# A planned one-core matmul with tanh-gelu: next groups' needs first, another inner split in raw group two, P7 for P3 in group four

## The chip, the cores and the metric

The kernel runs on one core of one Trainium2 chip. The metric is device microseconds of one execution. Matrix products run on TensorE (PE, with PEld for its weight loads), element-wise work on VectorE (DVE) and ScalarE (ACT), and DMAs are issued by two queues: GpSimd's (POOL) for loads and SyncE's (SP) for stores. Operands lie in SBUF (the names `bR`, `aT`, `aD`, `stage`, `y`), products accumulate in eight PSUM banks (`acc`), and `k_unit`, `k_piece` and `park` are scratch in DRAM.

## The reference

```python
a, b: float32 [4096, 4096]
x = np.matmul(a, b)
out = 0.5 * x * (1 + np.tanh(np.sqrt(2 / np.pi) * (x + 0.044715 * x**3)))   # float32 [4096, 4096]
```

## The kernel before

**Tiling.** A and B are halved in both directions (quadrants 11, 12, 21, 22). The output is made in 16 groups: one of four row blocks of 512 rows (`mb`) with one of four column blocks of 512 columns (`nb`), in each of the four output quadrants. A group is a 2 x 2 block product with inner length 2048, done with seven products in place of eight (Winograd's form of Strassen's scheme). `P1` to `P7` are these products, all in fp16 with float32 sums: P1 and P2 make C11, P6 is added to P1, P7 and P5 complete C22, P4 completes C21, P3 completes C12. A plain product is four quarters of 16 matmuls of 128x512. A product can be cut: the same scheme is applied once more inside it, in seven parts of 256 columns and four stages (`split`, `stage`, `part_pe`, lines 973 to 1093). That takes fewer matmul cycles, and more sums on DVE and copies on ACT.

**Stages.** Group 0 is written out by hand. Groups 1 to 5 (`raw_group`, line 1424) read B from the input; `RAW_CUT` (line 97) says which products of each are cut: P3 in 1, 2 and 4, P7 in 5. Group 3 also turns to the next row block: it loads A's next rows in eight pieces, transposes them on DVE and squares each row on ACT with an accumulator (`turn_quad`, line 1249, the squares at line 1272) for a check of the inputs' sizes. Groups 6 to 15 run in pairs (`late_pair`) with all products cut. The squares of B's quadrants for the same check (`square`, line 1303: ACT at 1316, DVE at 1321) are made where `SQUARES` (lines 2002 and 2003) has the group and quadrant.

**Banks and buffers in a raw group.** X is the first four PSUM banks, Y the last four. After P6 each bank of X is copied to SBUF (`u2`, by `copy_out`, line 1230), and then P7 is accumulated on it. With P7 plain, `u3` copies it again, adds Y and sends C22 out. With P7 cut, P4 goes to Y alone and alternates with P7's stages, and `p7_out` (line 1571) reads each X bank twice: with `u` for C21 and with `v` into a new small buffer for C22. Gelu runs on ACT (`out_of`, line 1214), the store on SP (`store_out`, line 1219), and the buffer returns to the list. `new_small` takes the buffer that has been in the list longest; ten of them rotate in the raw groups. If both P7 and P3 are cut, `raw_group` returns P3 (`third`), and the next group alternates its four stages with the four quarters of its P1.

**Order.** Nothing is issued directly. `Plan.add` records each operation with its engine, a duration out of a table, what it reads and writes, and a due time: the planned PE time plus `slack`, moved ahead of those that depend on it (`Plan.keys`). `front` is the number of the first matmul group (one `add` on PE) that needs the operation's result. `Plan.schedule` (line 236) then walks through time. PE's order is fixed; every other engine takes, of the operations that are ready, the one with the least

```python
(not x.size and x.front > n_pe + FRONT, x.key, x.n)
```

where `n_pe` is the number of PE groups started and `size` is set for DMAs alone. Before it takes an operation, it looks for one that becomes ready while that one would run and that is due sooner (`near`). `emit` then issues all in the planned order, so each engine's queue is fixed when the program is built.

Of the kernel before, what the change touches and what calls it, by code (L numbers as in the profile page):

```python
# [93 lines left out]

N_RAW = 6
RAW_MAKES = {}
RAW_CUT = {1: "P3", 2: "P3", 4: "P3", 5: "P7"}
GROUPS = {
    6: modes_of(m="P1 P2 P3 P4 P5 P6 P7"),
    7: modes_of(m="P1 P2 P3 P4 P5 P6 P7"),  # L100
# [10 lines left out]
FROM_INPUT = ((0, "P2"), (1, "P1"), (1, "P2"), (1, "P3"), (2, "P3"), (3, "P3"))  # L111
OWN = True
TEMPS = ()
SLACK = 60.0
TURN_PLAN = (("11", "11", "P1", None), ("21", "12", "S4", None), ("12", "S1", "P5", None), ("22", "S2", "next", "P1"))
BEHIND = 4
FRONT = 0
CASTS = {4: ((1, 'P3'), (2, 'P3')), (8, 'P5'): ((0, 'P2'),)}
CAST_SLACK = 60.0
TURN_PLAN = (("11", "11", "P1", None), ("21", "12", "S4", None), ("12", "S1", "P5", None), ("22", "S2", "next", "P1"))  # L120
BEHIND = 4
FRONT = 0
CAST_BACK = 17
SLACK2 = 18.0
TURN_SLACK = 18.0
FILL_SLACK = 60.0
TURN_PLAN = (("11", "11", "P1", None), ("21", "12", "S4", None), ("12", "S1", "P5", None), ("22", "S2", "next", "P1"))
BEHIND = 4
FRONT = 0
CASTS = {4: ((1, 'P3'), (2, 'P3')), (8, 'P5'): ((0, 'P2'),)}  # L130
CAST_SLACK = 60.0
TURN_PLAN = (("11", "11", "P1", None), ("21", "12", "S4", None), ("12", "S1", "P5", None), ("22", "S2", "next", "P1"))
BEHIND = 4
FRONT = 0
CAST_BACK = 17
SLACK2 = 18.0
PARK = (6, 8, 10, 12, 14)
TURNS = {6: 2, 10: 3}
ORDER = "10 11 70 71 20 21 60 61 50 51 30 31 40 41"
# [17 lines left out]
class Plan:  # L157

    def __init__(self):
        self.ops, self.state, self.now = [], {}, BUSY["PE"]  # L160

    def add(self, eng, dur, fn, r=(), w=(), size=0, batch=None, after=(), slack=18.0, weight=1.0, every=None):
        o = Op()
# [72 lines left out]
    def schedule(self):  # L236
# [23 lines left out]
        while n_done < len(self.ops):  # L260
            best, at = None, 1e30
            if n_pe < len(pe) and not pe[n_pe].left:
                at = max(free["PE"], pe[n_pe].ready)
                best = "PE"
            for e in engines:
                if ready[e] and out.get(e, 0) < LANES:
                    t = max(free[e], min(o.ready for o in ready[e]))
                    if t < at:
                        best, at = e, t
            ended = self.next_move(at)  # L270
            if ended is not None:
                o, q = ended
                out[q] -= 1
                if o is not None:
                    o.end = self.moved + 0.4
                    finish(o)
                if out[q] == LANES - 1:
                    free[q] = max(free[q], self.moved + 0.4)
                continue
            assert best is not None  # L280
            if best == "PE":
                o = pe[n_pe]
                n_pe += 1
# [67 lines left out]
def half_path(  # L351
# [15 lines left out]
    W = 2 * NC  # L367
# [653 lines left out]
    def stage(z, k):  # L1021
# [38 lines left out]
        elif k == 3:  # L1060
            part_pe(z, "6")
            if z.last and not z.base:
                x6 = z.sum.pop("6")
                z.sum["3"] = inner_sum(-1, x12, as_inner(x6), x6)
            j2 = new_small()
            for r in range(2):
                copy_part(j(j2, r), of("21", r))
            part_pe(z, "7")
            for r in range(2):
                add_part(of("12", r), of("12", r), j(j2, r))  # L1070
            free_small.append(j2)
            for r in range(2):
                add_part(of("22", r), of("21", r), j(z.j5, r))
            free_small.append(z.j5)
# [142 lines left out]
    def store_out(gi, i, ih, jh, f):  # L1217
        r0, c0 = place(gi, i, ih, jh)
        dma("SP", out[r0 : r0 + P, c0 : c0 + NC], sm(f), [("f", f)], [], "out")
        free_small.append(f)  # L1220

    def out_from(gi, i, ih, jh, s):
        f = new_small()
# [25 lines left out]
    def turn_quad(mb, quad, slot, pairs, own=False, after=()):  # L1249
# [3 lines left out]
        for h in range(2):  # L1253
# [21 lines left out]
                    [] if own else toks, [("rows", ih), *(toks if own else [("f", f)])], batch=("w", mb, quad, h),  # L1275
                    slack=SLACK)
            if not own:
                free_small.append(f)
# [145 lines left out]
    def raw_group(gi, keep_units, makes, fetch=(), next_nb=None, turn=None, pending=None):  # L1424
# [164 lines left out]
        if "P7" in cut:  # L1589
# [41 lines left out]
    def more_smalls():  # L1631
        for x in EXTRA:
            free_cells.remove(x)
            for h in range(2):
                f = len(small)
                small.append(cell(x)[:, h * W : (h + 1) * W].bitcast(F32))
                free_small.append(f)
# [43 lines left out]
    def late_pair(ga, turn):  # L1681
# [64 lines left out]
        def split_pair(name, done):  # L1746
# [46 lines left out]

            def join(hw, f):
                into_bank(f, *of(hw[:2], int(hw[2])))
                free_small.append(f)

            def ended(hw, r):
                done(*of(hw, r))
# [129 lines left out]
        def p4_done(w, i):  # L1929
# [15 lines left out]
            for h in range(2):  # L1945
# [9 lines left out]
            free_small.append(f)  # L1955

        def park():
            for w, i in BANKS:
                f = u[w, i]
                dma("SP", parked[w][i][:, :], sm(f), [("f", f)], [("park", w, i)], "out")  # L1960
                free_small.append(f)

        def unpark():
            for w, i in BANKS:
# [9 lines left out]
        if last:  # L1974
            final_answer()
        both("P2", is_cut("P2"), p2_done)
        both("P6", is_cut("P6"), p6_done)
        if last:
            final_read()
# [14 lines left out]
        new_a("P4")  # L1994
        if turn:
            new_a("next")
            at.update(new, S1=at["S3"], S2=at["22"])
# [115 lines left out]
```

## Time and profile before

| | us |
|---|---|
| median of 3 runs | 1457.21 |
| lowest, highest | 1456.33, 1457.86 |
| profiled execution, its own time | 1458.38 |
| its span, first to last instruction | 1456.8 |

The mean granted clock of the profiled execution is 0.998. In the page, a group row gives the line, the engine, the operation, out<-in by the program's names, the count, then busy us and mean ns of one, then the engine's idle time before it and what ended most of it. Lines are those of helpers where a helper records the operation: all DMAs of the plan are at L822, all sums at L916, plain matmuls at L596, those of cut products in raw groups at L1001 and in pairs at L1780. The "chain" is the work that ended last, followed back in time. By that chain the group 1 starts at some 123 us, group 2 at 215, group 3 at 310, group 4 at 412, group 5 at 507, and the pairs at 604.

### The profile page before, as it was taken

To read this page: it belongs to the slowest core of one execution; us is meant where nothing else is said; L and a number is where in the kernel's file an instruction comes from. 1 tells how busy PE (TensorE), PEld (TensorE's weight loads), DVE (VectorE), ACT (ScalarE), POOL (GpSimd) and SP (SyncE) were. 2 spreads that over 40 slices of the span, in tenths; PEclk is the share of its full clock that TensorE was granted. 3 is DMA by queue.
4 is the path that set the end of the run, shared out by engine and by line. 5 is a ranking of instruction groups with operands and counts; after the bars stand their busy time and mean duration, and the time that the engine had idled before them with its cause. 6 is when DMAs were issued, how large, how long until landed. Compare 5 with 4: busy or idle time off the path is not lost.

```text
span 1456.8 us, 19885 instructions
## 1 busy us (share of the span) xinstructions
PE 1442.1 (99%) x6878; PEld 673.2 (46%) x6878; DVE 1192.0 (82%) x1280; ACT 698.3 (48%) x1460; POOL 488.3 (34%) x892
## 2 busy tenths in 40 slices
PE   8999999999899999999999999999999999999998
PEld 3444454454344545544444444444444444444443
DVE  2499987948477779889998989888999899887887
ACT  5546764553983543462554513435473623343133
POOL 7775351343334522341413343213232212221220
PEclk9999999999999999999999999999999999999999
DMA  9999999999999998998989899969998866875763
GB/s 170 196 196 240 311 270 267 236 292 253 208 222 268 231 312 231 256 281 286 287 320 307 264 295 326 288 227 310 257 347 270 275 257 218 319 265 199 272 251 125
DMA packets 205244, 378.91 MB, mean 260 GB/s; under 512 B 21073, under 2 KB 115793, under 8 KB 205137
## 3 DMA queue, kind: packets, MB, share of 16 engines
q0 software_dynamic: 146816, 245.42, 69.5%
q1 hardware_dynamic: 58320, 132.15, 24.2%
q8 instruction: 56, 0.92, 0.2%
q14 instruction: 52, 0.42, 0.1%
HBM read 333.45 MB, written 138.42 MB: 324 GB/s over the span
## 4 chain that ended last, share of the span: by engine, by line
PE 92%; DMA 3%; POOL 2%; ACT 1%; issue 1%; DVE 0%; DVEq 0%; ACTq 0%; POOLq 0%
PE acc L1780 58%; PE acc L596 31%; PE acc L1001 3%; DMA stage<-in_a_dram 2%; DMA bR<-in_b_dram 1%; POOL bR L498 1%; POOL stage L498 1%; ACT y L1272 1%; POOL aD L498 0%; PE acc L631 0%; DMA bR<-k_unit 0%; ACT y L1230 0%; DMA aD<-in_a_dram 0%; DVE bR L916 0%; DVE y L610 0%
## 5 line engine op out<-in xcount | busy, mean ns | idle before, releaser
L1780 PE MATMUL acc<-bR 128*128 128x512 f16 x1536 | 339.4, 379 | 1.4 <-DVE bR L916 1.4
L916 DVE TENSOR_TENSOR bR<-bR 128x2048 f16<-128x2048 f16 (+1 forms) x155 | 258.1, 1681 | 48.4 <-PE acc L1780 16.1
L822 POOL DMA_DIRECT2D bR<-k_unit x234 | 127.2, 545 | 468.6 <-PE acc L1780 358.4
L1780 PEld LDWEIGHTS <-bR 128*128 128x128 f16 x1776 | 173.7, 98 | 211.2 <-issue 1.7
L596 PE MATMUL acc<-bR,aT 128*128 128x512 f16 x1152 | 254.3, 381 | 2.5 <-ACT y L1230 2.5
L1780 PE MATMUL acc<-bR,aT 128*128 128x512 f16 x1008 | 223.6, 379 | 0.0
L822 POOL DMA_DIRECT2D bR<-in_b_dram x256 | 138.3, 546 | 214.8 <-DVE stage L916 74.9
L1780 PEld LDWEIGHTS <-aT 128*128 128x128 f16 x1344 | 131.5, 98 | 158.6
L596 PE MATMUL acc<-bR,aD 128*128 128x512 f16 x896 | 195.0, 379 | 1.9 <-ACT y L1230 1.9
L1792 ACT COPY acc<-acc 128x512 f32<-128x512 f32 x140 | 79.8, 570 | 241.8 <-PE acc L1780 221.2
L1236 DVE TENSOR_TENSOR y<-acc,y 128x512 f32<-128x512 f32 x239 | 158.5, 684 | 41.0 <-PE acc L1780 17.1
L596 PEld LDWEIGHTS <-aT 128*128 128x128 f16 x1216 | 119.3, 98 | 144.4 <-issue 5.3
L596 PEld LDWEIGHTS <-aD 128*128 128x128 f16 x992 | 96.9, 98 | 119.8 <-issue 2.9
L1316 ACT ACTIVATE y<-bR 128x1024 bf16<-128x1024 f16 x128 | 128.0, 1048 | 43.3 <-DVE y L1321 32.6
L1780 PE MATMUL acc<-bR,aD 128*128 128x512 f16 x624 | 138.4, 379 | 0.0
L1214 ACT ACTIVATE y<-y 128x512 f32<-128x512 f32 x156 | 95.5, 628 | 73.1 <-DVE y L1236 72.6
L1780 PEld LDWEIGHTS <-aD 128*128 128x128 f16 x784 | 76.7, 98 | 92.5
L1321 DVE TENSOR_TENSOR y<-y 128x1024 bf16<-128x1024 bf16 x120 | 81.6, 686 | 36.8 <-ACT y L1316 33.8
L1789 ACT COPY y<-acc 128x512 f32<-128x512 f32 x99 | 57.9, 585 | 93.9 <-PE acc L1780 84.7
L471 DVE STREAM_TRANSPOSE aT<-stage 128x1024 uint32<-128x1024 uint32 (+1 forms) x41 | 52.0, 1301 | 47.2 <-DMA stage<-in_a_dram 43.2
L1780 PE MATMUL acc<-stage,aT 128*128 128x512 f16 x336 | 75.6, 379 | 0.0
L1241 DVE TENSOR_TENSOR acc<-acc,y 128x512 f32<-128x512 f32 x100 | 68.7, 692 | 6.4 <-ACT y L1789 5.8
(120 smaller groups left out, 1579.1 us busy)
## 6 DMA issues: line engine op xcount, KB each, us to landing
bR<-k_unit POOLq DMA_DIRECT2D x234, 512.0 KB, 7.5
out_dram<-y SPq DMA_DIRECT2D x204, 256.0 KB, 7.3
bR<-in_b_dram POOLq DMA_DIRECT2D x352, 128.0 KB, 7.0
k_unit<-bR SPq DMA_DIRECT2D x76, 512.0 KB, 7.0
stage<-in_a_dram POOLq DMA_DIRECT2D x96, 256.0 KB, 8.8
stage<-k_unit POOLq DMA_DIRECT2D x46, 512.0 KB, 8.1
k_unit<-stage SPq DMA_DIRECT2D x28, 512.0 KB, 5.5
out_dram<-bR SPq DMA_DIRECT2D x46, 256.0 KB, 7.6
```

The lines of the kernel that those rows point to most:

```text
L471: nc.vector.transpose(dst[:, :, x, :], src)
L596: nc.tensor.matmul(acc, sa[:, j // 2, i * P : (i + 1) * P, j % 2], sb[:, j, :], start=start and j == 0, stop=stop and j == 3, skip_group_c ...
L822: return plan.add(queue, COST[queue], lambda: eng.dma_start(out=dst, in_=src), r=r, w=w, size=MOVE[what] * SPREAD, weight=weight, **kw)
L916: nc.vector.tensor_tensor(out=dst, in0=xa, in1=ya, op=ALU.add if op > 0 else ALU.subtract)
L1214: act("gelu", lambda: nc.scalar.activation(t, t, ACT.Gelu_apprx_tanh), [("f", f)], [("f", f)])
L1236: dve("add", lambda: nc.vector.tensor_tensor(out=sm(g), in0=bank(s, i), in1=sm(f), op=ALU.add), [("f", f)], [("f", g), ("p", s, i)])
L1241: dve("add", lambda: nc.vector.tensor_tensor(out=bank(s, i), in0=bank(s, i), in1=sm(f), op=ALU.add), [("f", f)], [("p", s, i)])
L1316: act("square", lambda t=t, src=src: nc.scalar.activation(t, src, ACT.Square), [c(cx)], [("f", f)], slack=60.0)
L1321: dve("add16", lambda t=t, u=u: nc.vector.tensor_tensor(out=u, in0=u, in1=t, op=ALU.add), [("f", f)], [("f", e)], slack=60.0)
L1780: nc.tensor.matmul(bank(w, i), sa[:, jx // 2, r * P : (r + 1) * P, jx % 2], bv[:, jx, :], start=p in "17" and jx == 0, stop=jx == NJ - 1, ...
L1789: act("copy", lambda: nc.scalar.copy(out=sm(f), in_=bank(w, i)), [("p", w, i)], [("f", f)])
L1792: act("copy", lambda: nc.scalar.copy(out=bank(*dst), in_=bank(*x)), [("p", *x)], [("p", *dst)])
```

## The change

Which products are cut: group 2 cuts P7 and P3, group 4 cuts P7 and no more P3. Since both are cut in group 2, its P3 runs within group 3. The order: `FRONT` is 2, so operations that one of the next three matmul groups needs go ahead of others; `near` also takes an operation that the next group needs (`NEAR = 0`) while the chosen one isn't needed by then; slacks and the place of the cast loads (`CAST_BACK`) have other values. The squares of B's quadrant 21 move from group 4 to group 3. `new_small` can lend halves of operand cells when the list is empty; `LEND` is empty, and `drop_small` stands in place of the plain return to the list. Constants that stood several times stand once.

```diff
-RAW_CUT = {1: "P3", 2: "P3", 4: "P3", 5: "P7"}
+RAW_CUT = {1: "P3", 2: "P7 P3", 4: "P7", 5: "P7"}
...
-SLACK = 60.0
+SLACK = 90.0
...
-FRONT = 0
+FRONT = 2
+LEND = ()
+SQUARES_3 = ("12", "21")
+NEAR = 0
...
-CAST_BACK = 17
-SLACK2 = 18.0
-TURN_SLACK = 18.0
+CAST_BACK = 9
+SLACK2 = 20.0
+TURN_SLACK = 12.0
...
     def halves(self, toks):
+        toks = [self.alias.get(t[:2], t) for t in toks]
...
-                o = min((x for x in ready[best] if x.ready <= at),
-                        key=lambda x: (not x.size and x.front > n_pe + FRONT, x.key, x.n))
+                def rank(x):
+                    return not x.size and x.front > n_pe + FRONT, x.key, x.n
+
+                o = min((x for x in ready[best] if x.ready <= at), key=rank)
                 if not o.size:
-                    near = [x for x in ready[best] if at < x.ready < at + o.dur and x.key < min(o.key, at + o.dur)]
+                    near = [
+                        x for x in ready[best] if at < x.ready < at + o.dur
+                        and (x.key < min(o.key, at + o.dur) or x.front <= n_pe + NEAR < o.front)
+                    ]
                     if near:
-                        o = min(near, key=lambda x: (x.key, x.n))
+                        o = min(near, key=rank)
                         at = max(at, o.ready)
...
-    def new_small():
+    lent = {}
+
+    def new_small(lend=False):
+        own = [f for f in free_small if f in lent]
+        if lend and own:
+            free_small.remove(own[0])
+            return own[0]
+        if not free_small or lend and len(free_cells) > 1:
+            x = new_cell()
...
         return free_small.pop(0)
+
+    def drop_small(f):
+        if f in lent and lent[f][1] in free_small:
+            free_small.remove(lent[f][1])
+            free_cells.append(lent[f][0])
+        elif f in lent:
+            free_small.append(f)
+        else:
+            free_small.insert(len([x for x in free_small if x not in lent]), f)
...
-            f = new_small()
+            f = new_small(i in LEND)
             add_bank(v[i], X, i, f)
             out_of(gi, i, 1, 1, f)
...
-            run(fourth, stages_of(split(X, s3, here(s12), True), p7_out))
+            if "P4" in cut:
+                run(fourth)
+                run(stages_of(split(X, s3, here(s12), True), p7_out))
+            else:
+                run(fourth, stages_of(split(X, s3, here(s12), True), p7_out))
...
             if "P3" in cut:
                 for i in range(RT):
                     add_bank(u[i], Y, i)
+                if turn:
+                    free_cells.extend(SB)
                 run(p4(X, False, p4_out), third())
+                if turn:
+                    for x in SB:
+                        free_cells.remove(x)
+                p4_ends()
                 load_next("12", "21")
...
-    SQUARES |= {(3, "12")} | {(4, q) for q in ("11", "21", "22", "end")}
+    SQUARES |= {(3, q) for q in SQUARES_3} | {(4, q) for q in ("11", "21", "22", "end") if q not in SQUARES_3}
```

More of the change, by code (lines that the diff above doesn't have):

```diff
@@ L113 @@
 TEMPS = ()
-SLACK = 60.0
+SLACK = 90.0
 TURN_PLAN = (("11", "11", "P1", None), ("21", "12", "S4", None), ("12", "S1", "P5", None), ("22", "S2", "next", "P1"))
 BEHIND = 4
-FRONT = 0
+FRONT = 2
+LEND = ()
+SQUARES_3 = ("12", "21")
+NEAR = 0
 CASTS = {4: ((1, 'P3'), (2, 'P3')), (8, 'P5'): ((0, 'P2'),)}
 CAST_SLACK = 60.0
-TURN_PLAN = (("11", "11", "P1", None), ("21", "12", "S4", None), ("12", "S1", "P5", None), ("22", "S2", "next", "P1"))
-BEHIND = 4
-FRONT = 0
-CAST_BACK = 17
-SLACK2 = 18.0
-TURN_SLACK = 18.0
-FILL_SLACK = 60.0
[L127 to L136, printed above, removed]
+CAST_BACK = 9
+SLACK2 = 20.0
+TURN_SLACK = 12.0
+FILL_SLACK = 60.0
 PARK = (6, 8, 10, 12, 14)
@@ L159, in __init__ @@
     def __init__(self):
-        self.ops, self.state, self.now = [], {}, BUSY["PE"]
+        self.ops, self.state, self.now, self.alias = [], {}, BUSY["PE"], {}
     def add(self, eng, dur, fn, r=(), w=(), size=0, batch=None, after=(), slack=18.0, weight=1.0, every=None):
@@ L845, in new_chunk @@
         return x
-    def new_small():
-        return free_small.pop(0)
+    lent = {}
[6 more added lines that the diff above has]
+            x = new_cell()
+            for h in range(2):
+                f = len(small)
+                small.append(cell(x)[:, h * W : (h + 1) * W].bitcast(F32))
+                plan.alias["f", f] = ("c", x, h)
+                free_small.append(f)
+            lent[f], lent[f - 1] = (x, f - 1), (x, f)
+            if lend:
+                return free_small.pop()
+        return free_small.pop(0)
+    def drop_small(f):
[3 more added lines that the diff above has]
+        elif f in lent:
+            free_small.append(f)
+        else:
+            free_small.insert(len([x for x in free_small if x not in lent]), f)
     def sm(f):
@@ L1070, in stage @@
                 add_part(of("12", r), of("12", r), j(j2, r))
-            free_small.append(j2)
+            drop_small(j2)
             for r in range(2):
                 add_part(of("22", r), of("21", r), j(z.j5, r))
-            free_small.append(z.j5)
+            drop_small(z.j5)
             z.prepare(3)
@@ L1219, in store_out @@
         dma("SP", out[r0 : r0 + P, c0 : c0 + NC], sm(f), [("f", f)], [], "out")
-        free_small.append(f)
+        drop_small(f)
     def out_from(gi, i, ih, jh, s):
@@ L1277, in turn_quad @@
             if not own:
-                free_small.append(f)
+                drop_small(f)
         if (mb, ih) in seen_rows:
@@ L1636, in more_smalls @@
                 small.append(cell(x)[:, h * W : (h + 1) * W].bitcast(F32))
-                free_small.append(f)
+                drop_small(f)
                 for r in range(2):
@@ L1795, in join @@
                 into_bank(f, *of(hw[:2], int(hw[2])))
-                free_small.append(f)
+                drop_small(f)
             def ended(hw, r):
@@ L1954, in p4_done @@
                 dma("SP", out[r0 : r0 + P, c0 + h * HC : c0 + (h + 1) * HC], t, [("f", f, h)], [], "out_half")
-            free_small.append(f)
+            drop_small(f)
         def park():
@@ L1960, in park @@
                 dma("SP", parked[w][i][:, :], sm(f), [("f", f)], [("park", w, i)], "out")
-                free_small.append(f)
+                drop_small(f)
         def unpark():
@@ L1976, in late_pair @@
         both("P2", is_cut("P2"), p2_done)
+        new_a("P2")
         both("P6", is_cut("P6"), p6_done)
@@ L1996, in late_pair @@
             new_a("next")
+            assert len(new) == 4
             at.update(new, S1=at["S3"], S2=at["22"])
```

## The prediction

> **What bounds the kernel now.** I read the profile page first, then the waits of PE, then the chain of waits, then busy time by stretches.
>
> ```profile
> span 1456.8 us, 19885 instructions
> PE 1442.1 (99%) x6878; PEld 673.2 (46%) x6878; DVE 1192.0 (82%) x1280; ACT 698.3 (48%) x1460; POOL 488.3 (34%) x892
> PE 92%; DMA 3%; POOL 2%; ACT 1%; issue 1%; DVE 0%; DVEq 0%; ACTq 0%; POOLq 0%
> ```
>
> PE is the bound: busy 99% of the span and 92% of the chain. So the time can fall in two ways only: fewer PE cycles, or fewer PE stops. The stops are few, and the waits of PE name all of them (engine, line, releaser, us in total, times, longest):
>
> ```profile
> PE acc L596 <- ACT y L1230: 4.4, 2, 2.5
> PE acc L631 <- DMA bR<-in_b_dram: 2.2, 2, 1.3
> PE acc L605 <- DVE table L777: 1.5, 1, 1.5
> PE acc L1780 <- DVE bR L916: 1.4, 1, 1.4
> ```
>
> The second and third rows lie in the hand-written first group, which is not edited. The first is the one that the change aims at. The chain shows what happens there: ACT's copies of a finished PSUM bank (L1230) stand behind row squares (L1272, a square and an accumulator read to each).
>
> ```profile
> 366.59 0.73 ACT y L1272 x2
> ...
> 369.61 0.59 ACT y L1230
> ...
> 370.24 8.81 PE acc L596 x40
> ...
> 386.27 0.59 ACT y L1230
> ...
> 386.91 99.30 PE acc L596 x452
> ```
>
> PE restarts right behind the fourth copy, twice, at 370.24 and 386.91. Both places are in group 3, at the ends of P6 and P7 (u2 and u3 in the code). By stretches (length, PE, PEld, DVE, ACT, POOL busy, granted clock, DMA):
>
> ```profile
> 363.00:371.00 8.00, 6.06 (x29) 2.70 (x28) 3.86 (x4) 7.69 (x19) 4.13 (x8) 1.00 0.94 177
> 379.00:387.00 8.00, 5.47 (x26) 2.32 (x24) 4.61 (x7) 7.74 (x21) 2.75 (x5) 0.98 0.85 133
> 386.90:390.10 3.20, 3.19 (x8) 1.13 (x8) 2.65 (x3) 3.17 (x7) 2.49 (x5) 0.50 0.70 82
> ```
>
> PE is idle 8.00 - 6.06 = 1.94 and 8.00 - 5.47 = 2.53 us. ACT is busy 7.7 of 8 us in both. After the second stop the granted clock is 0.50 for 3.2 us, which costs 3.2 x 0.5 = 1.6 us; after the first it stays at 1.00.
>
> **The change, part by part.**
>
> *P7 of group 2 is split as well; in group 4 P7 is split in place of P3.* A split product next to a plain one, in the chain:
>
> ```profile
> 287.66 1.96 PE acc L1001 x16
> ...
> 293.07 3.49 PE acc L1001 x32
> ...
> 306.96 3.49 PE acc L1001 x32
> ...
> 590.52 13.81 PE acc L596 x64
> ```
>
> A plain product is 64 matmuls, 13.81 us. A split one is the first row and three pieces of 3.49, of which the first and the last are shown: 1.96 + 3 x 3.49 = 12.43 us. Group 2 gains one split: -1.4 us. Group 4 exchanges one for one: 0.
>
> What it adds elsewhere for one split: 8 operand sums on DVE (four of A, four of B), 4 half-bank adds, and 8 full-bank adds more (C21 and C22 are finished by two adds of each bank rather than one, and P4 goes to the other bank). The group-5 split shows their length:
>
> ```profile
> L916 DVE TENSOR_TENSOR bR<-bR 128x2048 f16<-128x2048 f16 x4 | 4.9, 1224 | 1.3 <-PE acc L1001 1.2
> L1236 DVE TENSOR_TENSOR y<-acc,y 128x512 f32<-128x512 f32 x17 | 11.2, 687 | 2.9 <-PE acc L596 1.6 <-DMA out_dram<-y 0.9 <-PE acc L1001 0.2
> L1019 DVE TENSOR_TENSOR acc<-acc,y 128x256 f32<-128x256 f32 x4 | 1.4, 422 | 0.0
> ```
>
> 8 x 1.22 + 8 x 0.69 + 4 x 0.42 = 17.0 us. The moved check (quadrant 21 of B, squared in group 3 and no more in group 4) adds 8 ACT squares and 7 DVE adds to group 3; six such adds take 4.59 us at 589.14 below, so 7 x 0.77 = 5.4 us. The groups 2, 3 and 4 are these stretches:
>
> ```profile
> 214.90:310.20 95.30, 95.30 (x499) 48.52 (x497) 76.97 (x91) 48.39 (x66) 31.07 (x59) 1.00 0.98 259
> 310.20:411.70 101.50, 97.03 (x443) 43.48 (x441) 54.56 (x57) 68.06 (x141) 34.62 (x62) 0.98 1.07 249
> ```
>
> P3 of group 2 is now carried into group 3 (its four stages alternate with the four quarters of P1), so the 22.4 us fall on 77.0 + 54.6 = 131.6 us of DVE work in 196.8 us: 154.0, or 78%. On average DVE hides it; without that cover it would be up to 22.4 us. Group 4 only takes 8 full-bank adds more and loses 7 of the check: near 0, hidden under plain P3, 13.81 us, which there follows the split P7.
>
> *Where the cover does run out: the end of split P7 in group 2.* The same code already runs in group 5. DVE and SP there, in order of time:
>
> ```profile
> 587.93 1.29 DVE L1236 TENSOR_TENSOR y<-acc,y 128x512 f32<-128x512 f32 x2 [0.18 <-PE acc L1001]
> 589.14 4.59 DVE L1321 TENSOR_TENSOR y<-y 128x1024 bf16<-128x1024 bf16 x6
> 593.65 3.15 DVE L1236 TENSOR_TENSOR y<-acc,y 128x512 f32<-128x512 f32 x5
> 597.73 0.69 DVE L1236 TENSOR_TENSOR y<-acc,y 128x512 f32<-128x512 f32 x1 [0.93 <-DMA out_dram<-y]
> ...
> 589.31 1.00 SPq L822 DMA_DIRECT2D out_dram<-y  x2
> ```
>
> Each bank of X is added twice, and the second result needs a new small buffer. Ten small buffers rotate; u and v hold eight of them, so the third and fourth results wait until the first and second stores have landed: DVE idles 0.93 us "<-DMA out_dram<-y" at 597.73. In group 5 nobody cares, as 13.81 us of plain P3 on the other banks follow. In group 2 only the first part pair of carried P3 follows (1.96 us), then P1 of group 3 wants X again. Landing of the stores, from issue (min/median/max), for 280 to 325 us (the end of group 2) and for 575 to 604 us (group 5):
>
> ```profile
> DMA to landing us min/median/max: 6.0/8.3/11.5
> ...
> DMA to landing us min/median/max: 6.8/10.3/12.3
> ```
>
> The median is that of stores queued behind others; the first of a burst on an empty queue is near the minimum, so I take 6.4 us. Counted from the end of P7 (590.52 in group 5): the first store is issued at 589.31 - 590.52 = -1.21; it lands at 5.2. The hand-over to DVE and to PE is shown at 703 us:
>
> ```profile
> 703.09 0.42 issue
> 703.51 2.30 DVE bR L916
> 705.82 0.04 issue
> ```
>
> With 0.42 + 0.69 + 0.04 PE may write the third bank at 6.3; it stands there at 1.96 + 2 x 13.81/16 = 3.7. That is a stop of 2.6 us. For the fourth bank the second store counts: in group 5 it landed at 597.73 - 0.42 = 597.3, 1.2 us after the first (589.31 + 6.8 = 596.1), against 0.86 of PE work: 0.4 us more, 3.0 in all. Bounds: 0 if the buffers come free in time, and with the slowest store of group 5, 12.3, it is 3.0 + 5.9 = 8.9.
>
> *The order.* FRONT = 2 puts work that one of the next three matmul groups needs ahead of anything else, and the "near" rule lets an engine wait a moment for such work. In the built order of the changed program the four copies after P6 of group 3 stand in one row, and after P7 it is two copies, two row squares, two copies; in the old one four or five row squares stood ahead of the last copy. Four copies in a row take 4 x 0.59 = 2.4 us, less than the 3.45 us (13.81/4) in which PE finishes the four banks. So both stops go: 1.94 + 2.53 + 1.6 of clock, and 0.16 us with each stop (a last matmul counts 379 ns on the page where its slot is 13.81/64 = 216 ns): -6.4 us. The bounds are 0 and -6.4; the built order puts it at the latter.
>
> The row squares that were passed over come four copies, 2.4 us, later at most, and with them the buffers of A's transposes for group 4:
>
> ```profile
> 420.69 2.36 DVE L471 STREAM_TRANSPOSE aT<-stage 128x1024 uint32<-128x1024 uint32 x2
> ...
> 432.02 2.35 DVE L916 TENSOR_TENSOR aD<-aD,aT 128x2048 f16<-128x2048 f16 x2
> ```
>
> The last sums of A are ready at 434.4; group 4 begins at 411.7 and first needs them in its third product, at 411.7 + 2 x 13.81 = 439.3. The slack of 4.9 us covers it: 0.
>
> *POOL's queue.* Quadrant 22 of the next B is loaded once carried P3 has used the old one, so its 16 loads now stand behind the 8 loads of A for the turn. In the old run (issues on POOL):
>
> ```profile
> 319.47 0.54 POOL L822 DMA_DIRECT2D bR<-in_b_dram  x1 [1.12 <-DVE bR L916]
> ...
> 336.62 0.59 POOL L822 DMA_DIRECT2D stage<-in_a_dram  x1 [1.58 <-DMA bR<-in_b_dram]
> ...
> 361.03 2.37 DVE L471 STREAM_TRANSPOSE aT<-stage 128x1024 uint32<-128x1024 uint32 x2
> ```
>
> All 24 had landed by 361.0, when the last was transposed. In the new order the B loads are last; P6 of group 3 needs the first half at its start, 310.2 + 3 x 13.81 - 1.4 + 3.0 = 353.2, and the second at its third quarter, 13.81/2 later, 360.1. If the queue ends at the same 361.0, the second half is ready at 361.0 + 0.42 + 1.22 + 0.04 = 362.7, late by 2.6 us; if the queue ends 2.6 us sooner, by nothing. P4's first B half is now used up during P7 and no more after it, so the loads ahead in the queue can start sooner; I take a value near the lower end, 0.6. Other moved pieces (the cast units that start 8 matmul groups later, TURN_SLACK, SLACK, SLACK2) change due times only and touch loads whose buffers are ready long before: 0. The stop of 1.4 us at 704 is a fetch that the edit leaves as it is: it stays.
>
> *Sum:* -1.4 - 6.4 + 3.0 + 0.6 = -4.2 us against the profiled execution's 1458.38 us (span 1456.8). That execution is 1.17 us over the median of the runs, 1457.21, so I take the difference off the median: 1453.0.
>
> **Does the clock fall after the new stop?** Above, an idle time of 1.94 us left the clock at 1.00 and one of 2.53 was followed by 0.50. The new stop, 2.6 in one piece, is at this edge. If it falls, 1.6 us go, of which the short waits behind it (0.4 and 0.6) are swallowed in part: about +1.0, so 1454.0.
>
> The Trainium skill ("TensorE: Matmul & The Clock Gate", Part 1) says that the clock halves after at least one idle window of some 3.4 us; by it the new stop leaves the clock alone and 1453.0 stands. The trace differs: 2.53 us were followed by the half clock.
>
> **The rivals.**
> - *The new stop does not come* (second results find free buffers, or stores land near 3 us): 1457.2 - 1.4 - 6.4 = 1449.4. For it: in group 5 DVE itself lost only 0.93 us. Against: it lost them on the very add that PE would wait for.
> - *B's quadrant 22 is late in full*, 2.6 in place of 0.6: 1455.0. For it: DMA is busy all through 310 to 411 (share 1.07).
> - *Slower: the stores land late.* At the turn of group 2 to 3, POOL loads B and SP stores at once. At 12.3 us the stop is 8.9, the clock surely falls, 1.6: 1457.2 - 7.8 + 8.9 + 0.6 + 1.6 = 1460.5. It turns to a loss that can be told, over 2.9 us, from a first landing of about 11.9 us on. Against: minima of 6.0 and 6.8.
> - *The order does not bring what it says*: ACT is late for another reason, the old stops stay: 1457.2 - 1.4 + 3.0 + 0.6 = 1459.4, short of what can be told. Against: the built order.
>
> **How the numbers follow.** Forecast 1453.0: 0.42. With the clock's fall 1454.0: 0.23. No new stop 1449.4: 0.16. Quadrant 22 late 1455.0: 0.06. Late stores 1460.5: 0.08. Old stops stay 1459.4: 0.05. A measurement of this kernel can tell 0.2%, 2.9 us, from no change, so faster is below 1454.3. Faster: 0.42 + 0.16 + two thirds of 0.23 = 0.73; within: 0.08 + 0.06 + 0.05 = 0.19; slower 0.08. The range goes from just under the case without a stop, 1449.0, to the late quadrant with some of the clock's cost, 1456.0; it leaves out the last two, 0.13.
>
> **What would show it.** PE's waits on ACT L1230's successor gone; 48 matmuls more; a new wait of PE on DVE's bank add (the L1236 of before) at about 302 us, itself waiting for a store; the granted clock at 1.00 or one piece of 0.50 just behind it; a wait on an operand sum near 354 or none; the 1.4 us at about 700 still there. Wrong would be: waits on ACT copies in group 3, no wait at 302, or a wait over 5 us there.

## The result, and the profile after

| us | before | changed |
|---|---|---|
| median, runs side by side (22 each) | 1457.31 | 1453.62 |
| lowest, highest | 1455.19, 1459.89 | 1450.68, 1458.80 |
| profiled execution, its own time | 1458.38 | 1452.51 |
| its span | 1456.8 | 1451.0 |

The ratio is 0.9973, with a 95% interval of 0.9965 to 0.9981: 3.7 us less, where 4.2 were forecast. The spans of the two profiled executions lie 5.8 us apart.

Many lines of the code move by a few. In the changed kernel plain matmuls of raw groups are at L592 (before L596), cut ones at L1022 (L1001), cut products of the pairs at L1811 (L1780), bank adds at L1257 (L1236), copies of a bank at L1251 (L1230), row squares at L1293 (L1272), operand sums at L937 (L916), gelu at L1235 (L1214).

First the page of the changed kernel (span; busy time, share and instructions of each engine):

```profile
span 1451.0 us, 20002 instructions
PE 1439.6 (99%) x6926; PEld 678.1 (47%) x6926; DVE 1203.2 (83%) x1308; ACT 695.5 (48%) x1460; POOL 486.7 (34%) x892
```

There are 48 matmuls more, as counted, and PE is still the bound. Its waits in the changed kernel (line, releaser, us in total, times, longest):

```profile
PE acc L592 <- DVE y L1257: 2.2, 2, 2.0
...
PE acc L1811 <- ACT acc L1823: 1.2, 1, 1.2
PE acc L1811 <- DVE bR L937: 1.2, 1, 1.2
```

The wait of 4.4 us on the copies is gone. In its place there are 2.2 us on a bank add and 1.2 us on a copy of ACT in the pairs. The sum over the profiled executions:

| place | us |
|---|---|
| one split more in group 2, by its pieces | -1.4 |
| stops on the copies in group 3, with the half clock | -6.4 |
| new stop at 302 us (2.2, and 0.16 for each of its two pieces) | +2.5 |
| new stop at 1071 us | +1.2 |
| waits in the first group, which the edit leaves alone (2.2 + 1.5 before, 1.5 after) | -2.2 |
| all else | +0.5 |
| difference of the spans | -5.8 |

The wait of 2.2 us in the first group is on a load of B (L631, now L627). The edit leaves that group alone, yet this wait is missing in the changed kernel and 0.3 to 1.2 us in the runs below, so it is taken as chance. Without it 3.6 are left, and the medians differ by 3.7.

The chain of waits of the changed kernel, through P7 of group 2 (from 271.97) and the new stop (start, us, what):

```profile
271.97 1.96 PE acc L1022 x16
...
277.38 3.49 PE acc L1022 x32
...
292.91 0.64 ACT y L1235
...
293.56 6.05 DMA out_dram<-y
...
300.32 0.68 DVE y L1342
301.00 0.61 DVE y L1257
...
301.66 1.02 PE acc L592 x4
```

The pieces of the cut P7 are as long as in group 5, so the -1.4 stands. The stop has two pieces, and the chain ends with the short one. PE's and DVE's timelines show where the long one ended (start, us, instruction, idle time before it):

```profile
300.46 1.02 PE L592 MATMUL acc<-bR,aT 128*128 128x512 f16 x4 [2.00 <-DVE y L1257]
```

```profile
299.71 0.69 DVE L1257 TENSOR_TENSOR y<-acc,y 128x512 f32<-128x512 f32 x1 [0.92 <-DMA out_dram<-y]
```

PE starts P1 of group 3 again at 300.46, after 2.00 us, when DVE has made the add that frees the third bank of X. DVE could begin this add only when a store had landed, issued at 293.56 and 6.05 us under way. Its small buffer was the add's target. The add of the fourth bank then stood behind a sum of the check on DVE (L1342), and PE waited 0.17 us more, until 301.66. The granted clock stayed at 1.00 behind this stop (length, PE, PEld, DVE, ACT, POOL busy, clock, DMA share):

```profile
298.00:303.00 5.00, 2.82 (x16) 1.31 (x14) 4.08 (x7) 3.36 (x6) 2.04 (x5) 1.00 1.13 285
```

The copies after P6 of group 3, and the last two after P7, on ACT's timeline of the changed kernel (start, us, instruction, idle time before it):

```profile
354.81 0.63 ACT L1293 ACTIVATE y<-stage 128x512 f16<-128x512 f16 x1
...
362.41 0.59 ACT L1251 COPY y<-acc 128x512 f32<-128x512 f32 x1 [6.88 <-PE acc L592]
363.27 0.59 ACT L1251 COPY y<-acc 128x512 f32<-128x512 f32 x1 [0.28 <-DMA k_unit<-bR]
364.13 0.59 ACT L1251 COPY y<-acc 128x512 f32<-128x512 f32 x1 [0.28 <-PE acc L592]
365.05 0.58 ACT L1251 COPY y<-acc 128x512 f32<-128x512 f32 x1 [0.33 <-PE acc L592]
...
378.95 1.05 ACT L1251 COPY y<-acc 128x512 f32<-128x512 f32 x2
```

The four copies after P6 stand in a row, as the built order said. But ACT had been idle for 6.88 us before them. It did not pass the row squares over; all sixteen were done at 355.5, and there was nothing to pass. In the kernel before, the second eight of them were held up until 361.01 by a load of A, and seven of these then stood among the copies, all ahead of the last one at 369.61. ACT's timeline of the kernel before, where that begins:

```profile
361.01 0.63 ACT L1272 ACTIVATE y<-stage 128x512 f16<-128x512 f16 x1 [1.66 <-DMA stage<-in_a_dram]
```

After P7 two squares do stand between the second copy and the third, as the built order said. They are early enough too: the last two copies begin at 378.95 (the last one of the kernel before: 386.27), and PE does not wait for them.

POOL's timeline of the changed kernel shows why the squares were early:

```profile
315.81 2.29 POOL L818 DMA_DIRECT2D stage<-in_a_dram  x4 [1.52 <-DVE acc L1040]
318.62 2.28 POOL L818 DMA_DIRECT2D stage<-in_a_dram  x4 [0.52 <-PE acc L1022]
325.26 0.55 POOL L818 DMA_DIRECT2D bR<-in_b_dram  x1 [4.37 <-ACT y L1235]
```

The eight loads of A are issued at 315.8 to 320.9, ahead of quadrant 22 of B. Before, the first of them was issued at 336.62, behind it.

### The profile page after: what moved, and what is told of

The parts are those of the page before. It is cut to its first block, busy times and chain, and to the rows that moved or that the text cites. A ratio compares the mean times of both kernels' runs of the same rounds, so it can differ in the third digit from the quotient of the medians.

```text
span 1451.0 us, 20002 instructions
## 1 busy us (share of the span) xinstructions
PE 1439.6 (99%) x6926; PEld 678.1 (47%) x6926; DVE 1203.2 (83%) x1308; ACT 695.5 (48%) x1460; POOL 486.7 (34%) x892
## 4 chain that ended last, share of the span: by engine, by line
PE 92%; DMA 4%; POOL 2%; issue 1%; DVE 1%; ACT 0%; DVEq 0%; ACTq 0%; POOLq 0%
PE acc L1811 58%; PE acc L592 31%; PE acc L1022 4%; DMA stage<-in_a_dram 3%; POOL bR L494 1%; POOL stage L494 1%; POOL aD L494 0%; DMA out_dram<-y 0%; DMA bR<-k_unit 0%; DMA bR<-in_b_dram 0%; DMA aD<-in_a_dram 0%; DVE bR L937 0%; DVE y L1257 0%; ACT stage L503 0%; DVE aD L577 0%
## 5 line engine op out<-in xcount | busy, mean ns | idle before, releaser
L1811 PE MATMUL acc<-bR 128*128 128x512 f16 x1536 | 339.5, 379 | 2.4 <-ACT acc L1823 1.2
L937 DVE TENSOR_TENSOR bR<-bR 128x2048 f16<-128x2048 f16 (+1 forms) x159 | 262.2, 1669 | 39.3 <-PE acc L1811 22.4
L1811 PEld LDWEIGHTS <-bR 128*128 128x128 f16 x1776 | 173.8, 98 | 212.3 <-issue 3.0
L592 PE MATMUL acc<-bR,aT 128*128 128x512 f16 x1024 | 225.6, 379 | 2.2 <-DVE y L1257 2.2
L1811 PE MATMUL acc<-bR,aT 128*128 128x512 f16 x1008 | 223.6, 379 | 0.0
L592 PE MATMUL acc<-bR,aD 128*128 128x512 f16 x960 | 208.8, 379 | 0.0
L1811 PEld LDWEIGHTS <-aT 128*128 128x128 f16 x1344 | 131.6, 98 | 158.5
L1257 DVE TENSOR_TENSOR y<-acc,y 128x512 f32<-128x512 f32 x255 | 168.5, 683 | 35.0 <-PE acc L1811 16.3
L1823 ACT COPY acc<-acc 128x512 f32<-128x512 f32 x140 | 79.8, 570 | 242.3 <-PE acc L1811 226.1
L592 PEld LDWEIGHTS <-aT 128*128 128x128 f16 x1088 | 106.5, 98 | 127.2 <-issue 2.7
L592 PEld LDWEIGHTS <-aD 128*128 128x128 f16 x1056 | 103.3, 98 | 124.5 <-issue 0.4
L1235 ACT ACTIVATE y<-y 128x512 f32<-128x512 f32 x164 | 100.5, 628 | 83.5 <-DVE y L1257 83.1
L1811 PE MATMUL acc<-bR,aD 128*128 128x512 f16 x624 | 138.4, 379 | 0.0
L1811 PEld LDWEIGHTS <-aD 128*128 128x128 f16 x784 | 76.6, 98 | 92.6
L1342 DVE TENSOR_TENSOR y<-y 128x1024 bf16<-128x1024 bf16 x120 | 81.6, 685 | 38.1 <-ACT y L1337 36.0
L1820 ACT COPY y<-acc 128x512 f32<-128x512 f32 x99 | 57.9, 585 | 94.6 <-PE acc L1811 86.6
L1811 PE MATMUL acc<-stage,aT 128*128 128x512 f16 x336 | 75.6, 379 | 0.0
L1251 ACT COPY y<-acc 128x512 f32<-128x512 f32 x60 | 34.8, 585 | 73.7 <-PE acc L592 55.3
```

Source lines behind the costliest of these rows:

```text
L592: nc.tensor.matmul(acc, sa[:, j // 2, i * P : (i + 1) * P, j % 2], sb[:, j, :], start=start and j == 0, stop=stop and j == 3, skip_group_c ...
L937: nc.vector.tensor_tensor(out=dst, in0=xa, in1=ya, op=ALU.add if op > 0 else ALU.subtract)
L1235: act("gelu", lambda: nc.scalar.activation(t, t, ACT.Gelu_apprx_tanh), [("f", f)], [("f", f)])
L1257: dve("add", lambda: nc.vector.tensor_tensor(out=sm(g), in0=bank(s, i), in1=sm(f), op=ALU.add), [("f", f)], [("f", g), ("p", s, i)])
L1342: dve("add16", lambda t=t, u=u: nc.vector.tensor_tensor(out=u, in0=u, in1=t, op=ALU.add), [("f", f)], [("f", e)], slack=60.0)
L1811: nc.tensor.matmul(bank(w, i), sa[:, jx // 2, r * P : (r + 1) * P, jx % 2], bv[:, jx, :], start=p in "17" and jx == 0, stop=jx == NJ - 1, ...
```

## The experiments

After this reading there were two explanations for the 6.4 us of group 3, and after the first four runs a third. One is the prediction's: the order rule (`FRONT`, `near`). The second: P3, carried into group 3, delays the loads of quadrant 22 behind those of A. The third says what the second acts on: squares and copies share small buffers. The eight row squares of a `stage` buffer all write an output that nobody reads (only the accumulator counts) into one small buffer; if a later copy gets the same buffer, it has to wait for all eight, whatever rule orders the engine.

The runs were made in three sittings, with the kernel before beside them each time: its median was 1458.06 us (24 runs) for the first four, 1457.64 (14) for the next four, 1457.53 (9) for the last two. Ratios are against these.

**The new order with the old cuts.**

```diff
 # changed kernel
-RAW_CUT = {1: "P3", 2: "P7 P3", 4: "P7", 5: "P7"}
+RAW_CUT = {1: "P3", 2: "P3", 4: "P3", 5: "P7"}
```

> The changed kernel with the old list of cuts (P3 in groups 1, 2 and 4, P7 in 5); all else as changed. Theory 1 (the prediction's): the order rule with FRONT = 2 removes the two stops on ACT's copies in group 3. Then PE's wait on the copies is gone here too, nothing new comes at 302 us, and the time is about 1457.3 - 6.4 = 1451. Theory 2: the stops went because carried P3 puts A's loads ahead of B's quadrant 22 on POOL, so that the row squares were done before the copies. Then they stay here: PE waits 4 to 6 us on ACT's copies in group 3, and the time is 1456 to 1459.

Measured: 1462.65 us (5 runs), ratio 1.0036 [1.0023, 1.0049]. It is slower than before: the stops stay, as the second explanation has it, but the time lies 3.7 us above its range. Its waits of PE, and two stretches:

```profile
PE acc L592 <- ACT y L1251: 7.3, 2, 4.1
```

```profile
363.00:373.00 10.00, 5.89 (x29) 2.60 (x27) 4.09 (x5) 9.44 (x24) 4.39 (x8) 1.00 0.92 188
373.10:376.50 3.40, 3.40 (x9) 1.22 (x8) 3.15 (x4) 3.34 (x7) 0.67 (x2) 0.50 1.15 204
```

With the whole rule in place the two stops are not gone but longer: 10.00 - 5.89 = 4.1 us and another of 3.2, each followed by 3.4 us at half clock. That is 7.3 + 2 x 1.7 = 10.7 us, against 6.0 in the kernel before (4.4 + 1.6), and the difference of 4.7 is about what the medians lose, 4.6. ACT's timeline in this kernel:

```profile
364.71 0.59 ACT L1251 COPY y<-acc 128x512 f32<-128x512 f32 x1
365.19 0.63 ACT L1293 ACTIVATE y<-stage 128x512 f16<-128x512 f16 x1
...
371.22 0.59 ACT L1251 COPY y<-acc 128x512 f32<-128x512 f32 x1
```

Eight squares stand between the third copy and the fourth, though the fourth is what PE waits for. The built instructions say why (ACT, in issue order, with the numbers of the small buffers; 85 and 86 are two loads of A):

```
order_new_cuts_old             changed kernel
L1293 y_100 <- stage_85  x7    L1293 y_97 <- stage_85  x8
L1251 y_89  <- acc_102         L1293 y_95 <- stage_86  x8
L1251 y_90  <- acc_103         L1251 y_98 <- acc
L1293 y_100 <- stage_85        L1251 y_87 <- acc
L1251 y_100 <- acc_104         L1251 y_97 <- acc
L1293 y_99  <- stage_86  x8    L1251 y_95 <- acc
L1251 y_99  <- acc_105
```

The third and fourth copies write buffers 100 and 99, and the sixteen squares write just these. The squares were recorded first, so no rule on order can put one of these two copies ahead of the squares that write its buffer. In the changed kernel it is the same (97 and 95), but there the squares are long done. In the kernel before it was again buffers 100 and 99.

**The old order with the new cuts.**

```diff
 # kernel before
-RAW_CUT = {1: "P3", 2: "P3", 4: "P3", 5: "P7"}
+RAW_CUT = {1: "P3", 2: "P7 P3", 4: "P7", 5: "P7"}
```

> The kernel before with the new list of cuts alone (P7 and P3 in group 2, P7 in 4); its order rule and slacks as before. Theory 1: the stops on ACT's copies stay (4.4 us and the half clock behind them), the stop at 302 us comes, PE work is 1.4 us less: 1457.3 - 1.4 + 2.4 = 1458.3. Theory 2: no wait of PE on the copies of group 3, a stop of 2 to 3 us at about 302: 1452 to 1454.

Measured: 1457.22 us (12 runs), 0.9996 [0.9987, 1.0004]. Its waits of PE, and the stretch behind the second of them:

```profile
PE acc L1780 <- DVE bR L916: 3.3, 2, 1.9
PE acc L596 <- DVE y L1236: 2.0, 1, 2.0
```

```profile
302.30:305.50 3.20, 3.11 (x12) 1.48 (x11) 3.20 (x4) 1.21 (x2) 1.11 (x3) 0.50 1.14 289
```

The stops on the copies are gone without any new rule, by the cuts alone, as the second explanation said; its time, 1452 to 1454, was missed by 3 us. Most of what the stops free is spent elsewhere: 2.0 us at the new stop, 1.6 us of half clock behind it, and a stop of 1.9 us at 661 us in the pairs that neither kernel has.

**The changed kernel without its order rule.**

```diff
 # changed kernel
-FRONT = 2
+FRONT = 0
...
-NEAR = 0
+NEAR = -100000
```

> The changed kernel with FRONT = 0 and the near rule's new half switched off (as before the change); cuts and slacks as changed. Theory 1: the stops on ACT's copies are back, 1453.6 + 6.4 = 1460. Theory 2: no wait on the copies, the stop at 302 stays, and the time is that of the changed kernel within 1.5 us.

Measured: 1453.04 us (6 runs), 0.9968 [0.9957, 0.998]: the changed kernel's time without the rule. Its longest wait and the stretch behind it:

```profile
PE acc L592 <- DVE y L1257: 3.3, 2, 3.1
```

```profile
303.00:306.40 3.40, 3.23 (x13) 1.60 (x12) 3.40 (x4) 1.17 (x2) 1.48 (x3) 0.51 1.12 315
```

ACT's timeline in this kernel, the first and the last copy after P6 of group 3:

```profile
365.56 0.59 ACT L1251 COPY y<-acc 128x512 f32<-128x512 f32 x1 [6.88 <-PE acc L592]
...
368.20 0.59 ACT L1251 COPY y<-acc 128x512 f32<-128x512 f32 x1 [0.33 <-PE acc L592]
```

The four copies stand in a row without the rule too, behind an ACT that was idle for 6.88 us, and PE does not wait for them. The new stop was longer here and the clock fell; the stop at 1071 us is missing. So the rule is worth nothing that these runs can tell. This kernel keeps the new slacks, the place of the cast loads, the moved check and smaller edits; the kernel with the old order and the new cuts lacks them, and is 4 us slower. Which of them makes the difference is not shown; the cast loads have a run below and make none.

**The loads alone.** In the kernel before, the loads of quadrant 22 for group 3 are recorded behind the first eight of A, with no other edit.

```diff
 # kernel before
-    behind = {}
+    behind, put_off = {}, []
...
         turn_quad(turn, "11", raw("21"), (24, 26))
+        while put_off:
+            put_off.pop()()
...
-            after()
+            if gi == 2:
+                put_off.append(after)
+            else:
+                after()
```

> The kernel before with one move: the loads of B's quadrant 22 for group 3 are recorded after A's first eight loads and no more ahead of them; cuts and order rule as before. Theory 1: the stops on the copies stay, 1457. Theory 2: they go, with the half clock (-6.4 us); instead PE may wait for quadrant 22 at the start of P6 of group 3, 0 to 2.6 us: 1451 to 1454, and no stop at 302, since P7 of group 2 is plain.

Measured: 1457.01 us (12 runs, 1454.02 to 1464.31), 0.9998 [0.9985, 1.001]. Its longest wait of PE, and the chain ahead of it:

```profile
PE acc L596 <- DVE bR L916: 2.5, 1, 2.5
```

```profile
347.54 4.76 DMA bR<-in_b_dram
...
352.47 1.23 DVE bR L916
```

Both stops on the copies are gone by the load order alone (the profiled execution is the fastest of the twelve). Quadrant 22 is then late: P6 waited 2.5 us for its sum. The profiled span is 4.3 us shorter than before (1452.5), but the runs scatter over 10 us, and their median gained nothing where 1451 to 1454 was expected. Why they scatter is not shown.

**The shared buffer alone.** In the kernel before, the row squares write over their own input, so that no copy shares a buffer with them. Order rule, cuts and loads are as before.

```diff
 # kernel before, turn_quad
-            f = None if own else new_small()
+            f = None
...
-                    s[:, x, :] if own else small[f].bitcast(F16)[:, : 2 * RUN], s[:, x, :], ACT.Square,
+                    s[:, x, :], s[:, x, :], ACT.Square,
...
-                    [] if own else toks, [("rows", ih), *(toks if own else [("f", f)])], batch=("w", mb, quad, h),
+                    [], [("rows", ih), *toks], batch=("w", mb, quad, h),
...
-            if not own:
-                free_small.append(f)
```

> The kernel before with one edit: the row squares of the turn write their (unused) squares over the stage they read, as they do in the pairs, and no more into a small buffer. Cuts, loads and order rule as before. Theory 3: the third and fourth copies after P6 and P7 of group 3 get the very small buffers into which the eight row squares of a piece write, so they cannot start before the last of those squares, whatever the order rule says. Then both stops go here (4.4 us, 0.3 of pipeline, 1.6 of clock), with nothing new at 302 or 350: about 1458 - 6.3 = 1451.5. If ACT's order or the late loads alone make the stops, they stay: 1457 to 1458.

Measured: 1452.33 us (5 runs), 0.9962 [0.9949, 0.9974], where 1451.5 was expected. These are the first three of its waits of PE, and part of ACT's timeline:

```profile
PE acc L605 <- DVE table L777: 1.5, 1, 1.5
PE acc L1778 <- DVE bR L916: 1.4, 1, 1.4
PE acc L631 <- DMA bR<-in_b_dram: 0.9, 2, 0.5
```

```profile
363.94 0.58 ACT L1230 COPY y<-acc 128x512 f32<-128x512 f32 x1
364.41 0.65 ACT L1272 ACTIVATE stage<-stage 128x512 f16<-128x512 f16 x1
365.04 0.63 ACT L1272 ACTIVATE stage<-stage 128x512 f16<-128x512 f16 x1
365.65 0.59 ACT L1230 COPY y<-acc 128x512 f32<-128x512 f32 x1
```

The squares are still late; two lie between the third copy and the fourth, and more follow. The last copy now begins at 365.65 rather than 369.61, and both stops are gone. This edit of a few lines brings 5.3 us to the old kernel (1457.64 - 1452.33), no less than the whole change.

**The new stop: two pieces of P3 first.** PE takes the first two parts of carried P3 before it comes back to the first bank of X.

```diff
 # changed kernel, raw_group
-            run(pending[0](), first)
+            t = pending[0]()
+            for fn in (t[0], t[1], first[0], first[1], t[2], first[2], t[3], first[3]):
+                fn()
```

> The changed kernel with one edit: where carried P3 of group 2 alternates with P1 of group 3, PE does P3's first two stages, then P1's first two quarters, then the rest in turn. That gives the stores of P7's results 3.5 us more before PE needs bank three of X. Theory: the stop at 302 us (2.2 us in the changed kernel's profile) is the wait for a small buffer under store; it goes, and the time is about 1453.6 - 2.4 = 1451. Rival (DVE itself is late there): a stop of 1 to 2 us stays.

Measured: 1450.53 us (6 runs), 0.9956 [0.9942, 0.997]. The stretch in which the stop had been:

```profile
296.00:303.00 7.00, 7.00 (x57) 5.23 (x55) 7.00 (x11) 5.50 (x12) 4.83 (x9) 1.00 1.20 242
```

PE runs through without a break. The ratio lies 0.0017 under that of the changed kernel, 2.5 us, the size of the stop, though the two intervals still overlap.

**The place of the cast loads.** The changed kernel with the old value.

```diff
-CAST_BACK = 9
+CAST_BACK = 17
```

> The changed kernel with CAST_BACK = 17 as before; the cast loads (16 DMAs for group 4's and group 8's casts) may start eight matmul groups sooner. The prediction put this at nothing. Rival: they take POOL's queue from a fetch in group 6, and PE stops there at about 650 to 662 us for 2 to 3 us (order_old_cuts_new has a stop of 1.9 at 661): 1456.

Measured: 1454.32 us (8 runs), 0.9972 [0.9962, 0.9982]: no difference that can be told. The waits show a fetch that is 0.8 us late, at 652 us, and the new stop at 1.8 us in its longest piece, with 3.4 us at half clock behind it (the stretch):

```profile
PE acc L592 <- DVE y L1257: 2.0, 2, 1.8
PE acc L1811 <- DMA bR<-k_unit: 0.8, 1, 0.8
```

```profile
302.00:305.40 3.40, 3.40 (x13) 1.75 (x13) 3.40 (x4) 1.64 (x2) 1.12 (x3) 0.50 1.14 288
```

**Group 4 with its old cut.**

```diff
 # changed kernel
-RAW_CUT = {1: "P3", 2: "P7 P3", 4: "P7", 5: "P7"}
+RAW_CUT = {1: "P3", 2: "P7 P3", 4: "P3", 5: "P7"}
```

> The changed kernel with P3 cut in group 4 as before, in place of P7. The prediction put the exchange at nothing: the time of the changed kernel, 1453.6, within 1.5 us, and no new wait of PE between 407 and 502 us. Rival: the exchange is part of the gain, 1455 or more.

Measured: 1452.20 us (5 runs), 0.9961 [0.9948, 0.9974]. The exchange of P7 for P3 brings nothing that shows. The first of its waits of PE:

```profile
PE acc L1811 <- ACT acc L1823: 2.7, 2, 2.4
```

The stop at 1071 us is 2.4 us long here. It varies with edits that lie far away from it.

**Other buffers for the second results of group 2.** With free halves of operand cells in place of the small buffers that wait for a store, and PE's order left alone.

```diff
 # changed kernel, p7_out
-            f = new_small(i in LEND)
+            f = new_small(gi == 2)
```

> The changed kernel with one edit: the four C22 results of P7 in group 2 get lent halves of operand cells and no buffer under store. The small-buffer theory: the stop at 302 us goes (2.2 us). The cells lent are out of use for the stores' 6 to 8 us, which may put off the sums of carried P3 and quadrant 22's loads: a new stop of 0 to 3 us at about 350: 1451 to 1454. Rival (DVE late): the stop at 302 stays at 2 us.

Measured: 1451.52 us (5 runs), 0.9954 [0.994, 0.9967]. The wait that is new in it:

```profile
PE acc L592 <- DVE bR L937: 0.9, 1, 0.9
```

No wait on a bank add is left, so it was the buffer under the store and not a busy DVE that stopped PE at 302 us. The long piece of that stop also follows the first store's time to landing: 5.7 us and a stop of 1.6 with group 4's old cut, 5.8 and 1.8 with the old place of the cast loads, 6.05 and 2.0 in the changed kernel, 7.1 and 3.1 without the order rule. With the lent buffers, 0.9 us come back at 350 us, where quadrant 22 is now late.

**Both at once.** The changed kernel with two pieces of P3 first and with squares over their own input (the diffs above).

> The changed kernel with both edits: carried P3's first two stages ahead of P1's quarters, and row squares written over their stage. The small-buffer theory sees no stop of PE left between 90 and 690 us in either kernel, so the second edit has nothing to win here: the time of third_two_ahead, 1450.5, within 1.5 us, the lowest of all. If something else of the changed kernel waits for those buffers (the copies of the pairs near 1071 us), it is 1 us lower.

Measured: 1450.89 us (5 runs, 1449.53 to 1452.01), 0.9948 [0.9935, 0.9962]. Its interval lies below that of the changed kernel, so it is the faster one. It can't be told from the version with P3's pieces alone, which fits: once the loads are early, the shared buffer costs nothing that shows. In its profile quadrant 22 is late by 1.3 us.

## Why the prediction was right, and where it was not

- *PE work, -1.4.* Right: 48 matmuls more, and the pieces as long as forecast. DVE has the 28 instructions more that were counted, and in groups 2 to 4 PE waits for nothing but the stop at 302 us.
- *The order, -6.4.* The size was right and the step wrong. It said that "both stops go" because `FRONT` and `near` put the copies ahead of the squares, and took the built order of the changed program as evidence. But the four copies stand in a row without the rule too, and with the rule and the old cuts the stops remain. In its place: copies three and four wait for the buffers into which the squares dump their output (the run with squares in place shows it by itself), and carried P3 puts A's loads ahead of quadrant 22, so that the squares are done 7 us before the copies after P6 begin. The quoted rows had the clue: squares and copies both write `y`. And the step on POOL's queue had the cause, but booked it as a cost alone.
- *The new stop, +3.0.* Right in place and kind: a second result that waits for a store's buffer. It measured 2.2 us in two pieces, 2.0 and 0.2. The forecast's pieces were 2.6 and 0.4. In the first, 0.35 us is the store, 6.05 rather than 6.4, and 0.3 the hand-over to DVE, 0.1 (299.61 to 299.71) rather than 0.42. The second was booked on the second store, but what stood before the add was a sum of the check.
- *Quadrant 22, +0.6.* 0 in the changed kernel's profile; 0.9 with the lent buffers, 1.3 with both edits at once, and 2.5 where the loads alone were moved. The mechanism is there; how late the quadrant comes depends on the other edits.
- *Edits at nothing.* Right for group 4 and for the cast loads, by their own runs; the stop near 700 us stayed, at 1.2. `SLACK`, `SLACK2`, `TURN_SLACK` and the moved check were not tried one by one. The kernel with the old order and the new cuts lacks them, has a stop of 1.9 us at 661 us and is 4 us slower than the one without the rule, so together with the smaller edits they may well be worth something.
- *Not foreseen:* the stop of 1.2 us in the pairs. ACT's timeline of the changed kernel there, and its chain:

```profile
1069.09 0.59 ACT L1820 COPY bR<-acc 128x512 f32<-128x512 f32 x1 [0.85 <-DMA out_dram<-bR]
```

```profile
1070.22 0.69 DVE y L1257
...
1070.93 0.63 ACT y L1235
...
1072.18 0.49 ACT acc L1823
1072.71 7.50 PE acc L1811 x34
```

The copy that PE needed (L1823) came behind a gelu and a row square. The gelu began when an add of DVE (1070.22) ended, and ACT, which had lost 0.85 us to a buffer under a store, came free at nearly the same time. With group 4's old cut and with the lent buffers, where this stop is 2.4 and 1.5 us, the chain runs through that store (7.5 and 7.9 us under way). This reading rests on the traces; no run took that wait away by itself.

- *The sum.* -4.2 forecast, -3.7 measured: the stop was 0.5 us shorter all told and quadrant 22 cost nothing, and 1.2 came in the pairs. That the total fits so well is in part luck: these misses cancel, and the largest term was earned by the early loads and not by the rule that it was booked on.
- *Rivals.* Late stores (12.3 us) did not show: the landing was 6.05. The clock fell behind the new stop in three of the other kernels (without the order rule, old order with new cuts, cast loads at their old place), though not in the changed kernel's profile, so giving it a chance of its own was right. "The order does not bring what it says" was half right: the rule does not, and the stops went all the same.

Open: whether it is the rule or the slacks that make the old cuts slower with the new order than with the old one; no run separates them. How it comes about, ACT's timeline shows. This is the first copy after P6 of group 3 in the kernel with the new order and the old cuts:

```profile
362.61 0.59 ACT L1251 COPY y<-acc 128x512 f32<-128x512 f32 x1 [6.92 <-PE acc L592]
```

Two copies stand ahead of the last nine squares in ACT's queue, so ACT was idle for 6.92 us, although all eight loads of A had landed by some 359 us (issued by 340.6, 18.6 us under way at most). Then eight squares had to run between the third copy and the fourth; in the kernel before it was five. Putting the first copies ahead made the last one later, since that one needs the squares that were passed over.

## What to carry to other kernels

When an engine does work in an order that no rule would choose, look at what both instructions write before blaming the rule: an output that nobody reads still makes its buffer busy, and a wait behind work on the same engine shows as no wait at all. A built order shows what will stand where, not which edit put it there; building it once more with that edit undone tells it. And when a step is booked as "a transfer comes later", ask at once what comes earlier in its place.

## What the runs showed of the hardware

The half clock lasted some 3.4 us each time, but what sets it off is not the length of the stop alone. It followed stops of 1.8 (cast loads at their old place), 2.0 (old order with new cuts), 2.5 (kernel before), 3.1 (without the order rule), 3.2 and 4.1 us (new order with old cuts). It did not follow others of 1.6 and 2.4 (group 4's old cut), 1.94 (kernel before), 2.0 (changed kernel) and 2.5 (the loads alone). So from 1.8 to 2.5 us it may come or not, at a price of 1.6 to 1.7 us. What decides it stays open. The Trainium skill ("TensorE: Matmul & The Clock Gate", Part 1) says that the clock drops after at least one idle window of some 3.4 us and is full again after a busy window of the same length. These runs agree with the second, as each slow stretch lasted some 3.4 us, and not with the first.
